# Earlier squares of the next block, paired log-sigmoids and two wide exponent activations in a hybrid attention, mLSTM and GLA layer

## The chip, the cores and the metric

The kernel runs on one core of one Trainium2 chip. The metric is device time in microseconds (us). Three runs of the kernel before gave 1427.89, 1430.01 and 1431.16 us; the median, 1430.01 us, is the time before.

## The reference

One layer over 2048 rows of width 1024. The rows are normalised (RMSNorm) and projected once; the columns of the projection feed three head groups, whose outputs are multiplied by gates, concatenated, projected back and added to the input. A last RMSNorm follows.

```python
hn = rmsnorm(x, norm_g)
z = einsum('bsd,de->bse', hn, w_in)
# A) softmax attention over a band of 9 chunks, with a relative-position bias
# B) mLSTM: exponential input gate, sigmoid forget gate, running-max stabiliser
lf = log_sigmoid(f_pre);  bcum = cumsum(lf)          # within a chunk
inter_log = bcum + m_prev
m_row = max(inter_log, max_j(log_d))
d_mat = exp(log_d - m_row);  inter_w = exp(inter_log - m_row)
den = max(abs(den), exp(-m_row))
# C) gated linear attention with a decay per key channel
log_alpha = log_sigmoid(ga @ w_alpha + b_alpha) / 16
```

What matters here are two log-sigmoids and a handful of exponentials. The forget gates of the six mLSTM heads are 6 rows (partitions) of numbers along time; the decays of GLA are 128 rows. From the forget and input gates come four rows per head, kept in one tile `rows`: gate minus cumulated decay, the weight of each key up to its chunk's end, exp(-m), and the weight of the old state.

## The kernel before, in words

The sequence is cut into 4 blocks of 512 rows (`q` = 0 to 3). The first phase, up to about 1005 us, does for each block the projections, mLSTM and GLA; the second phase does attention and the output projection. All the change is in the first phase.

For each block the order of projections is: `gq` and `gk` for GLA (`proj_z`), the row tiles of v (`proj_v`, eight of them, the first four with line 402 to 405 as their evacuation), the GLA gate, the mLSTM q and k, the mLSTM gates, then the nine attention tiles (`proj_a`). Each tile of a projection is 24 matmuls of 512 columns into one PSUM bank; there are two such banks (`ip`), so tile n+2 waits until tile n is copied out. Weights are read by DMA, split into a rounded part (line 235, ScalarE) and a rest (line 236, VectorE or GpSimd).

Between these matmuls smaller chains of work are woven in. They are generators with the names prep, gates, gla_in, gla and mlstm. Every `yield pe, gap` says how much TensorE time the piece before takes and how long the next piece should stay away; `flow.piece` hands out pieces at every half tile. This sets the order on TensorE, which is fixed by hand. The order on the other engines is set by a scheduler, which may put an instruction as early as its buffers and inputs allow, so that a line's place in the program isn't its place on its engine. Each engine then works strictly in its own order: one instruction that waits holds up all behind it.

The chains that the change touches:

- prep, for the next block: loads x in four tiles `xraw` (line 284), squares and sums them (line 285, ScalarE), forms the reciprocal root (286, 287) and a diagonal matrix (290), yields with a gap of 14, broadcasts it with a matmul (293), copies that (295), loads x transposed (299), scales it (302), and takes the gate columns with eight matmuls (309) into `g1` (314). The `xraw` tiles are four, shared by both loads.
- split_x: rounded part and rest of x for the projections (323, 324).
- gates: matmul 331 brings the 6 + 6 gate rows, line 272 to 276 (`log_sigmoid`) turn the forget rows into log-sigmoids: absolute value, minimum with 0, exp, ln(1 + .), difference. Scans follow (337 for the running maximum, 341 for the sums within a chunk), then the rows (342 to 353), the last of them by eight activations of one chunk each with a bias (352, 353). Then matmul 362 brings the 128 GLA rows, which pass through the same `log_sigmoid` into `ls`. After a gap, four transposes (369) read all of `rows`.
- gla_in: line 608 on, exponentials and scans of `ls`; they need `ls` and `zg`.

ScalarE reads its functions from a table that it has to load: exp and ln alternate here, and the loads stand as rows of their own, ACT_TABLE_LOAD.

In the text, B0 to B3 are the starts of the four blocks, and T1 to T4 the first four row tiles of v there. The two tiles ahead of T1 are gq (copied out by line 422) and gk (copied out by line 423).

Of the kernel before, what the change touches and what calls it, by code (L numbers as in the profile page):

```python
# [8 lines left out]
FP32 = mybir.dt.float32  # L9
FR = mybir.dt.float32r  # L10
AF = mybir.ActivationFunctionType
ALU = mybir.AluOpType
# [4 lines left out]
P = 128  # L17
D = 1024
KT = D // P
QT = 512  # L20
ST = 256
L = 128
NC = QT // L
AH, MH, GH = 6, 6, 4
# [3 lines left out]
G0 = 96  # L28
# [71 lines left out]
def f32(ap):  # L100
    return ap.bitcast(FP32)
# [3 lines left out]
def trunk_kernel(ctx: ExitStack, tc: tile.TileContext, xT, x, w_f, w_t, w_o, w_gates, norm_g, conv_w,  # L105
                 gate_sel, one_row, bias, ml_g, gla_g, final_g, out):
    nc = tc.nc
    S = x.shape[0]
    NQ = S // QT
# [23 lines left out]
    flow = Flow()  # L133
# [8 lines left out]
    with ExitStack() as pa_:  # L142
# [21 lines left out]
        gsel = one.tile([P, 2 * P], FP32, name="gsel")  # L164
# [3 lines left out]
        rows = one.tile([P, QT], FP32, name="rows")  # L168
# [44 lines left out]
        st = {"zb": None, "m": zero6, "S": None, "B": None}  # L213

        def g_tile(shape):
            return gpool.tile(shape, FP32, name="g")
# [50 lines left out]
                        flow.piece(12 * 0.227)  # L267
                evac(tt, ps)

        def log_sigmoid(dst, src, n):  # L270
            ab = g_tile([P, QT])[0:n] if n == P else g_tile([P, QT])[G0:G0 + n]
            nc.scalar.activation(ab, src, AF.Abs)
            nc.vector.tensor_scalar(dst, src, 0.0, None, op0=ALU.min)
            nc.scalar.activation(ab, ab, AF.Exp, scale=-1.0)
            nc.scalar.activation(ab, ab, AF.Ln, bias=1.0)
            nc.vector.tensor_tensor(dst, dst, ab, op=ALU.subtract)


        def prep(q, R):
            t0 = q * QT  # L280
            rs = big.tile([P, NC], FP32, name="rs")
            for tt in range(NC):
                xt = xraws.tile([P, D], FP32, name="xraw")
                nc.sync.dma_start(xt, x[t0 + tt * P:t0 + (tt + 1) * P, :])
                nc.scalar.activation(xt, xt, AF.Square, accum_out=rs[:, tt:tt + 1])
            nc.vector.tensor_scalar(rs, rs, 1.0 / D, EPS, op0=ALU.mult, op1=ALU.add)
            nc.gpsimd.tensor_tensor(rs, rs, mhalf[:, 0:NC], op=ALU.pow)
            dg = g_tile([P, NC, P])
            for tt in range(NC):
                nc.vector.tensor_scalar(dg[:, tt, :], ident, rs[:, tt:tt + 1], None, op0=ALU.mult)  # L290
            yield 0.0, 14.0
            rb = bank("pw")
            nc.tensor.matmul(rb, ones, dg.rearrange("p a t -> p (a t)"), start=True, stop=True)
            rbs = g_tile([P, QT])
            nc.scalar.copy(rbs, rb)
            raws = []
            for g in range(4):
                raw = xraws.tile([P, 2, QT], FP32, name="xraw")
                nc.sync.dma_start(raw, xT[:, 2 * g:2 * g + 2, t0:t0 + QT])
                for j in range(2):  # L300
                    k = 2 * g + j
                    nc.vector.scalar_tensor_tensor(raw[:, j, :], raw[:, j, :], ng[:, k:k + 1], rbs, op0=ALU.mult, op1=ALU.mult)
# [12 lines left out]
            R["raws"], R["g1"] = raws, g1  # L315
# [12 lines left out]
        def gates(q, g1, R):  # L328
            t0 = q * QT
            pb = bank("pw")  # L330
            nc.tensor.matmul(pb, gsel[:, P:2 * P], g1, start=True, stop=True)
            fm = g_tile([P, QT])[G0:G0 + MH]
            gi = g_tile([P, QT])[G0:G0 + MH]
            nc.vector.tensor_copy(gi, pb[32:32 + MH])
            log_sigmoid(fm, pb[0:MH], MH)
            mr = g_tile([P, QT])[G0:G0 + MH]
            nc.vector.tensor_tensor_scan(mr, fm, gi, st["m"], op0=ALU.add, op1=ALU.max)
            bc = g_tile([P, QT])[G0:G0 + MH]
            for c in range(NC):
                cs = slice(c * L, (c + 1) * L)  # L340
                nc.vector.tensor_tensor_scan(bc[:, cs], ones[G0:G0 + MH], fm[:, cs], 0.0, op0=ALU.mult, op1=ALU.add)
            nc.vector.tensor_tensor(rows[0:MH], gi, bc, op=ALU.subtract)
            nm = bc
            nc.vector.tensor_tensor(nm, bc, mr, op=ALU.subtract)
# [17 lines left out]
            nc.tensor.matmul(pa, gsel[:, 0:P], g1, start=True, stop=True)  # L362
            ls = big.tile([P, QT], FP32, name="ls", bufs=1)
            log_sigmoid(ls, pa, P)
            R["ls"] = ls
            yield 0.9, 13.0
            rt_ps = bank("pw")
            for c in range(NC):
                nc.tensor.transpose(out=rt_ps[:, c * P:(c + 1) * P], in_=rows[:, c * L:(c + 1) * L], identity=ident)
# [12 lines left out]
            yield 0.6, 1.0  # L382
# [351 lines left out]
        for q in range(NQ):  # L734
            st["q"] = q
            flow.need("gla_in")
            flow.need("gla")
            z = proj_z(X)
            vs, vg = proj_v(X)
            gg = proj_gg(X)  # L740
            flow.need("gates")
            G = {}
            flow.start("gla_in", gla_in(q, z, R["ls"], G))
            flow.start("gla", gla(q, vg, gg, G))
            flow.need("mlstm")
            qk = proj_m(X)
            M = dict(R)
            flow.start("mlstm", mlstm(q, qk, vs, M))
            M["gm"] = proj_gm(X)
            if q + 1 < NQ:  # L750
                flow.need("gla_in")
                R = {}
                flow.start("prep", prep(q + 1, R))
            proj_a(q, X)
            if q + 1 < NQ:
                flow.need("prep")
                X = split_x(R["raws"])
                flow.start("gates", gates(q + 1, R["g1"], R))
# [313 lines left out]
```

## Time and profile before

| | us |
|---|---|
| median of three runs | 1430.01 |
| the profiled execution, its own time | 1430.58 |
| its span in the trace | 1428.9 |
| TensorE busy | 1319.6 |
| VectorE busy | 788.7 |
| ScalarE busy | 616.5 |
| GpSimd busy | 606.5 |

The mean granted clock of TensorE is 0.953 of full speed. In rows of the profile PE is TensorE, PEld its weight loads, DVE is VectorE, ACT is ScalarE, POOL is GpSimd and SP the engine that issues most DMAs. A row of waits reads: engine, tile and line that waited, what ended the wait, total, how many times, the longest. A row of the timeline reads: start, duration, engine, line, operation, and in brackets the idle time ahead of it with what ended it.

### The profile page before, as it was taken

Reading aid. Unit: us, or ns where it says so; the run is one execution under the profiler, and the core shown is the slowest. Engines: PE = TensorE matmul, PEld = TensorE weight load, DVE = VectorE, ACT = ScalarE, POOL = GpSimd, SP = SyncE. Lnnn points to the kernel's source line nnn. Section 1 sums busy time; section 2 is a strip of 40 time slices with the busy share of each in tenths; the row PEclk is TensorE's granted clock in tenths of the full one; section 3 lists DMA queues with packets and bytes.
Section 4 is the critical chain, followed back from the end, with each engine's and each line's share of the span. In section 5 each row is a group of like instructions: output and inputs, shape, how many; then the busy total and the mean of one; then the engine's idle time right before and its main releaser. Section 6 shows DMA issues by size and latency. Waiting matters only on the chain.

```text
span 1428.9 us, 20086 instructions
## 1 busy us (share of the span) xinstructions
PE 1319.6 (92%) x7044; PEld 1064.9 (75%) x7044; DVE 788.7 (55%) x1874; ACT 616.5 (43%) x1173; POOL 606.5 (42%) x847
## 2 busy tenths in 40 slices
PE   5899989989998998999899899998878999999997
PEld 2678768867877876888677677787756887877876
DVE  6525556662664765265566527556556756656731
ACT  5634313463432347343224534321456555655531
POOL 4215762322576222266622325651245354454452
PEclk7999989999999999999999999997877999999999
DMA  7433214453421445432244533231587464555322
GB/s 245 152 112 117 74 54 131 133 177 111 118 74 56 130 140 177 125 111 74 67 124 121 156 118 93 73 110 49 148 241 229 130 184 133 179 161 160 99 67 89
DMA packets 107205, 180.10 MB, mean 126 GB/s; under 512 B 9824, under 2 KB 54752, under 8 KB 107104
## 3 DMA queue, kind: packets, MB, share of 16 engines
q1 hardware_dynamic: 102496, 170.43, 40.4%
q10 hardware_dynamic: 4608, 8.39, 1.6%
q8 instruction: 56, 0.92, 0.3%
q14 instruction: 45, 0.37, 0.1%
HBM read 143.14 MB, written 35.65 MB: 125 GB/s over the span
## 4 chain that ended last, share of the span: by engine, by line
PE 67%; DVE 12%; ACT 8%; DMA 6%; issue 4%; POOL 3%; SPq 0%; POOLq 0%; ACTq 0%; DVEq 0%
PE ip L243 11%; PE ip L245 10%; PE ip L244 10%; PE s L826 3%; PE ip L947 3%; PE ip L946 3%; PE ip L945 3%; PE ip L263 3%; PE ip L264 3%; PE ip L265 3%; PE tp L887 2%; DVE pt L840 2%; PE ga L673 2%; ACT w L235 2%; DVE qk L449 2%
## 5 line engine op out<-in xcount | busy, mean ns | idle before, releaser
L243 PE MATMUL ip<-x,w 128*128 128x512 f32 x800 | 326.7, 408 | 0.0
L244 PE MATMUL ip<-x,w 128*128 128x512 f32 x800 | 313.3, 392 | 1.2 <-DVE x L324 1.2
L245 PE MATMUL ip<-x,w 128*128 128x512 f32 x800 | 313.6, 392 | 0.0
L235 ACT CAST w<-wraw 128x1024 fp32r<-128x1024 f32 x132 | 138.3, 1049 | 193.9 <-PE ip L245 136.4
L236 DVE TENSOR_TENSOR w<-wraw,w 128x1024 fp32r<-128x1024 f32 x88 | 114.2, 1299 | 172.1 <-ACT w L235 170.0
L236 POOL TENSOR_TENSOR w<-wraw,w 128x1024 fp32r<-128x1024 f32 x44 | 106.1, 2410 | 217.5 <-ACT w L235 217.3
L243 PEld LDWEIGHTS ip<-x,w 128*128 128x128 f32 x800 | 150.9, 189 | 43.8 <-issue 11.9
L244 PEld LDWEIGHTS ip<-x,w 128*128 128x128 f32 x800 | 151.1, 189 | 32.8 <-DVE x L324 2.9
L245 PEld LDWEIGHTS ip<-x,w 128*128 128x128 f32 x800 | 150.7, 188 | 33.0
L845 POOL TENSOR_SCALAR pt<-pt,sm 128x640 f32<-128x640 f32 (+2 forms) x96 | 70.4, 735 | 148.8 <-DVE sm L844 118.1
L263 PE MATMUL ip<-w,x 128*128 128x512 f32 x256 | 105.5, 412 | 20.8 <-ACT zg L423 14.4
L264 PE MATMUL ip<-w,x 128*128 128x512 f32 x256 | 104.1, 407 | 4.6 <-POOL w L236 3.8
L945 PE MATMUL ip<-wo,y 128*128 128x512 f32 x256 | 107.0, 418 | 0.0
L843 ACT ACTIVATE pt<-pt,sm 128x640 f32<-128x640 f32 (+2 forms) x96 | 73.3, 764 | 71.0 <-DVE sm L840 68.0
L265 PE MATMUL ip<-w,x 128*128 128x512 f32 x256 | 103.3, 403 | 0.0
L947 PE MATMUL ip<-wo,y 128*128 128x512 f32 x256 | 101.7, 397 | 0.3 <-POOL y L853 0.3
L946 PE MATMUL ip<-wo,y 128*128 128x512 f32 x256 | 101.5, 396 | 0.0
L893 DVE TENSOR_TENSOR pl<-tp,ph 128x512 fp32r<-128x512 f32 (+2 forms) x126 | 74.6, 599 | 31.5 <-ACT ph L892 30.4
L826 PE MATMUL s<-kk,qq 128*128 128x384 f32 (+1 forms) x360 | 80.8, 333 | 10.7 <-DVE sm L840 9.2
L826 PEld LDWEIGHTS s<-kk,qq 128*128 128x128 f32 x360 | 60.6, 201 | 29.9 <-DVE sm L840 23.4
L633 POOL TENSOR_TENSOR prd<-gk,zg 128x16 f32<-128x16 f32 (+15 forms) x128 | 66.5, 520 | 33.4 <-PE pw L639 26.5
L892 ACT CAST ph<-tp 128x512 fp32r<-128x512 f32 (+2 forms) x126 | 63.1, 509 | 33.6 <-PE tp L887 32.4
(240 smaller groups left out, 2418.8 us busy)
## 6 DMA issues: line engine op xcount, KB each, us to landing
wraw<-in_w_f SPq DMA_DIRECT2D x100, 512.0 KB, 3.6
wraw<-in_w_t SPq DMA_DIRECT2D x32, 512.0 KB, 4.2
qq<-q_d SPq DMA_DIRECT2D x48, 256.0 KB, 4.5
kk<-k_d SPq DMA_DIRECT2D x18, 512.0 KB, 6.4
vv<-v_d SPq DMA_DIRECT2D x18, 512.0 KB, 7.3
xraw<-in_x SPq DMA_DIRECT2D x16, 512.0 KB, 4.6
xraw<-in_xT SPq DMA_DIRECT2D x16, 512.0 KB, 7.5
xr<-in_x SPq DMA_DIRECT2D x16, 512.0 KB, 3.7
```

What stands on the lines that cost most here:

```text
L235: nc.scalar.copy(w[:, :, 0, :], rv)
L236: other().tensor_tensor(w[:, :, 1, :], rv, f32(w[:, :, 0, :]), op=ALU.subtract)
L243: nc.tensor.matmul(ps, w[:, k, 0, :], X[k][:, 0, :], start=(k == 0), stop=False)
L244: nc.tensor.matmul(ps, w[:, k, 0, :], X[k][:, 1, :], start=False, stop=False)
L245: nc.tensor.matmul(ps, w[:, k, 1, :], X[k][:, 0, :], start=False, stop=(k == KT - 1))
L263: nc.tensor.matmul(ps, X[k][:, 0, t], w[:, 0, :], start=(k == 0), stop=False)
L264: nc.tensor.matmul(ps, X[k][:, 0, t], w[:, 1, :], start=False, stop=False)
L265: nc.tensor.matmul(ps, X[k][:, 1, t], w[:, 0, :], start=False, stop=(k == KT - 1))
L826: nc.tensor.matmul(sp[:, :cn], qq[:, l, tt * P:(tt + 1) * P], kk[:, ko + c0:ko + c0 + cn], start=(l == 0), stop=(l == 1))
L945: nc.tensor.matmul(ps, Y[k][:, 0, t], wo[k, j][:, 0, :], start=(e == 0), stop=False)
L946: nc.tensor.matmul(ps, Y[k][:, 0, t], wo[k, j][:, 1, :], start=False, stop=False)
L947: nc.tensor.matmul(ps, Y[k][:, 1, t], wo[k, j][:, 0, :], start=False, stop=(e == KT - 1))
```

## The change

Three edits. The part of prep up to the diagonal matrix becomes a function `prep_x` of its own, which is called for the next block ahead of the mLSTM projections instead of behind the mLSTM gates; prep then begins with the broadcast matmul, and its gap of 14 is gone. Both log-sigmoids of gates are taken together: both matmuls first, then the absolute values and exponentials of both, then both logarithms. The eight chunk activations become two of 512 columns: the chunk's bias is added before by VectorE with a broadcast operand (one addition for the key weights, two for the state weights), and three more rows are formed in a tile of their own and copied. The scheduler puts all of it in its own order.

```diff
-        def log_sigmoid(dst, src, n):
-            ab = g_tile([P, QT])[0:n] if n == P else g_tile([P, QT])[G0:G0 + n]
-            nc.scalar.activation(ab, src, AF.Abs)
-            nc.vector.tensor_scalar(dst, src, 0.0, None, op0=ALU.min)
-            nc.scalar.activation(ab, ab, AF.Exp, scale=-1.0)
-            nc.scalar.activation(ab, ab, AF.Ln, bias=1.0)
-            nc.vector.tensor_tensor(dst, dst, ab, op=ALU.subtract)
-        def prep(q, R):
+        def log_sigmoid(pairs):
+            for dst, src, ab in pairs:
+                nc.scalar.activation(ab, src, AF.Abs)
+                nc.vector.tensor_scalar(dst, src, 0.0, None, op0=ALU.min)
+                nc.scalar.activation(ab, ab, AF.Exp, scale=-1.0)
+            for dst, src, ab in pairs:
+                nc.scalar.activation(ab, ab, AF.Ln, bias=1.0)
+                nc.vector.tensor_tensor(dst, dst, ab, op=ALU.subtract)
+        def prep_x(q):
...
-            yield 0.0, 14.0
+            return dg
+
+        def prep(q, R, dg):
+            t0 = q * QT
+            yield 0.0, 0.0
...
             nc.vector.tensor_copy(gi, pb[32:32 + MH])
-            log_sigmoid(fm, pb[0:MH], MH)
+            nc.scalar.copy(fm, pb[0:MH])
+            yield 0.9, 3.0
+            pa = bank("pw")
+            nc.tensor.matmul(pa, gsel[:, 0:P], g1, start=True, stop=True)
+            ls = big.tile([P, QT], FP32, name="ls", bufs=1)
+            log_sigmoid([(ls, pa, g_tile([P, QT])), (fm, fm, g_tile([P, QT])[G0:G0 + MH])])
+            R["ls"] = ls
...
-            nc.vector.tensor_tensor(rows[0:MH], gi, bc, op=ALU.subtract)
             nm = bc
+            gb_ = gi
+            nc.vector.tensor_tensor(gb_, gi, bc, op=ALU.subtract)
+            nc.scalar.copy(rows[0:MH], gb_)
+            nc.scalar.activation(rows[64:64 + MH], mr, AF.Exp, scale=-1.0)
             nc.vector.tensor_tensor(nm, bc, mr, op=ALU.subtract)
             nc.scalar.copy(hl_nm[G0:G0 + MH], nm)
+            nc.vector.tensor_tensor(c4(gb_), c4(gb_), c4(nm)[:, :, L - 1:L].broadcast_to([MH, NC, L]), op=ALU.add)
+            nc.scalar.activation(rows[32:32 + MH], gb_, AF.Exp)
...
-            nc.scalar.activation(rows[64:64 + MH], mr, AF.Exp, scale=-1.0)
-            for c in range(NC):
-                cs = slice(c * L, (c + 1) * L)
-                mp = st["m"] if c == 0 else mr[:, c * L - 1:c * L]
-                nc.scalar.activation(iw[:, cs], nm[:, cs], AF.Exp, bias=mp)
-                nc.scalar.activation(rows[32:32 + MH, cs], rows[0:MH, cs], AF.Exp, bias=nm[:, (c + 1) * L - 1:(c + 1) * L])
+            nc.vector.tensor_tensor(iw[:, 0:L], nm[:, 0:L], st["m"].broadcast_to([MH, L]), op=ALU.add)
+            nc.vector.tensor_tensor(c4(iw)[:, 1:NC], c4(nm)[:, 1:NC], c4(mr)[:, 0:NC - 1, L - 1:L].broadcast_to([MH, NC - 1, L]),
+                                    op=ALU.add)
+            nc.scalar.activation(iw, iw, AF.Exp)
...
-            yield 0.9, 3.0
-            pa = bank("pw")
-            nc.tensor.matmul(pa, gsel[:, 0:P], g1, start=True, stop=True)
-            ls = big.tile([P, QT], FP32, name="ls", bufs=1)
-            log_sigmoid(ls, pa, P)
-            R["ls"] = ls
             yield 0.9, 13.0
...
-        flow.start("prep", prep(0, R))
+        flow.start("prep", prep(0, R, prep_x(0)))
         load_consts()
...
             flow.need("mlstm")
+            if q + 1 < NQ:
+                dg = prep_x(q + 1)
             qk = proj_m(X)
...
-                flow.start("prep", prep(q + 1, R))
+                flow.start("prep", prep(q + 1, R, dg))
```

How it moves instructions is read at three places. From here on lines of the changed kernel are called N and a number: N287 is before's 285 (squares), N341 the new copy of the 6 forget rows, N273, N275 and N277 are the absolute value, exp and ln of `log_sigmoid`, N278 its difference, N432 and N433 are before's 422 and 423, N414 is 404, N369 the last wide activation. In the rows as they stand below the letter is L in both.

First place: ScalarE at B1, from the squares to the copy of gk. Before:

```order
L285 ACTIVATE xraw,rs<-xraw 128x1024
L235 CAST w<-wraw 128x2x512
L422 ACTIVATE zg<-ip 128x512
L275 ACT_TABLE_LOAD
L275 ACTIVATE g<-g 6x512
L272 ACTIVATE g<-pw 128x512
L274 ACT_TABLE_LOAD
L274 ACTIVATE g<-g 128x512
L348 ACTIVATE rows<-g 6x512
L275 ACT_TABLE_LOAD
L275 ACTIVATE g<-g 128x512
L235 CAST w<-wraw 128x2x512
```

Line 423 follows. Now:

```order
L432 ACTIVATE zg<-ip 128x512
L287 ACTIVATE xraw,rs<-xraw 128x1024
L273 ACTIVATE g<-pw 128x512
L273 ACTIVATE g<-g 6x512
L275 ACTIVATE g<-g 128x512
L275 ACTIVATE g<-g 6x512
L277 ACT_TABLE_LOAD
L277 ACTIVATE g<-g 128x512
L277 ACTIVATE g<-g 6x512
L235 CAST w<-wraw 128x2x512
L433 COPY zg<-ip 128x512
```

One table load stands between the two copies where there were three; the 6-row absolute value and exp, which stood among the squares, now stand between the copies, and so does the fourth square. The squares themselves are where they were, behind split_x at the block's start. In the whole program the table loads are 9 where they were 17.

Second place: ScalarE just behind it, up to the end of the work on `rows`. Before, the last two of the eight chunk activations and what follows them:

```order
L352 ACTIVATE rows<-g 6x128
L353 ACTIVATE rows<-rows,g 6x128
L614 ACTIVATE qt<-lc 128x256 x2
L402 COPY vg<-ip 128x128
L404 CAST hl<-ip 128x3x64
```

Now:

```order
L359 ACTIVATE rows<-g 6x512
L412 COPY vg<-ip 128x128
L414 CAST hl<-ip 128x3x64
L628 ACTIVATE lc<-lc 128x256 x2
L358 COPY rows<-g 6x512
L674 COPY Qb<-qt 32x8x16 x4
L414 CAST hl<-ip 128x3x64
L361 CAST hl_nm<-g 6x512
L412 COPY vg<-ip 128x128
L363 ACTIVATE rows<-g 6x512
L414 CAST hl<-ip 128x3x64
L369 ACTIVATE rows<-rows 6x512
```

`rows` was complete ahead of the first copy of T1 (402); it now is complete behind the first copy of T2 (the second 412).

Third place: VectorE from the 6-row log-sigmoid on. Before, the 6-row chain was taken without a break:

```order
L276 TENSOR_TENSOR g<-g 6x512
L337 SCALAR_TENSOR_TENSOR g<-g,ml 6x512
L341 SCALAR_TENSOR_TENSOR g<-ones,g 6x128 x4
L273 TENSOR_SCALAR ls<-pw 128x512
L355 COPY ml<-g 6x1
L342 TENSOR_TENSOR rows<-g 6x512
```

Now, its head:

```order
L278 TENSOR_TENSOR g<-g 6x512
L622 SCALAR_TENSOR_TENSOR lc<-rst_153,ls 128x256 x2
L349 SCALAR_TENSOR_TENSOR g<-g,ml 6x512
L353 SCALAR_TENSOR_TENSOR g<-ones,g 6x128
L236 TENSOR_TENSOR w<-wraw,w 128x2x512
L353 SCALAR_TENSOR_TENSOR g<-ones,g 6x128 x3
L292 TENSOR_SCALAR g<-ident,rs 128x128 x4
```

Then come five short rows, N357 (before's 342), and this, up to the last addition to `rows`:

```order
L415 TENSOR_TENSOR hl<-ip,hl 128x3x64
L630 TENSOR_TENSOR qt<-zg,qt 128x256
L634 TENSOR_TENSOR Dt<-Dt,dl 128x2
L629 TENSOR_TENSOR lc<-lc,zg 128x256 x2
L360 TENSOR_TENSOR g<-g 6x512
L634 TENSOR_TENSOR Dt<-Dt,dl 128x2x2 x2
L415 TENSOR_TENSOR hl<-ip,hl 128x3x64
L362 TENSOR_TENSOR g<-g 6x512
L366 TENSOR_TENSOR rows<-g,ml 6x128
L367 TENSOR_TENSOR rows<-g 6x384
```

The GLA rows (622, 627, 630, 629: before's 612, 617, 620, 619), the split of a weight tile (236) and T1's copies (415, before's 405) now stand inside the 6-row chain, which has grown by three rows (362, 366, 367).

On TensorE the four transposes 369 stand where they stood, between T2 and T3. The broadcast matmul 293 and the gate matmuls 309 move some 14 us of modelled TensorE time earlier inside the block, and with them, on VectorE, the eight scalings 302.

More of the change, by code (lines that the diff above doesn't have):

```diff
@@ L268, in proj_t @@
                 evac(tt, ps)
-        def log_sigmoid(dst, src, n):
-            ab = g_tile([P, QT])[0:n] if n == P else g_tile([P, QT])[G0:G0 + n]
-            nc.scalar.activation(ab, src, AF.Abs)
-            nc.vector.tensor_scalar(dst, src, 0.0, None, op0=ALU.min)
-            nc.scalar.activation(ab, ab, AF.Exp, scale=-1.0)
-            nc.scalar.activation(ab, ab, AF.Ln, bias=1.0)
-            nc.vector.tensor_tensor(dst, dst, ab, op=ALU.subtract)
-        def prep(q, R):
+        def log_sigmoid(pairs):
+            abs_ = []
+            for dst, src, ab in pairs:
[6 more added lines that the diff above has]
+        def prep_x(q):
             t0 = q * QT
@@ L331, in gates @@
             nc.tensor.matmul(pb, gsel[:, P:2 * P], g1, start=True, stop=True)
+            gi = g_tile([P, QT])[G0:G0 + MH]
             fm = g_tile([P, QT])[G0:G0 + MH]
-            gi = g_tile([P, QT])[G0:G0 + MH]
             nc.vector.tensor_copy(gi, pb[32:32 + MH])
-            log_sigmoid(fm, pb[0:MH], MH)
+            nc.scalar.copy(fm, pb[0:MH])
[5 more added lines that the diff above has]
+            R["ls"] = ls
             mr = g_tile([P, QT])[G0:G0 + MH]
@@ L341, in gates @@
                 nc.vector.tensor_tensor_scan(bc[:, cs], ones[G0:G0 + MH], fm[:, cs], 0.0, op0=ALU.mult, op1=ALU.add)
-            nc.vector.tensor_tensor(rows[0:MH], gi, bc, op=ALU.subtract)
+            c4 = lambda t: t.rearrange("p (c t) -> p c t", t=L)
             nm = bc
+            gb_ = gi
+            nc.vector.tensor_tensor(gb_, gi, bc, op=ALU.subtract)
+            nc.scalar.copy(rows[0:MH], gb_)
+            nc.scalar.activation(rows[64:64 + MH], mr, AF.Exp, scale=-1.0)
             nc.vector.tensor_tensor(nm, bc, mr, op=ALU.subtract)
             nc.scalar.copy(hl_nm[G0:G0 + MH], nm)
+            nc.vector.tensor_tensor(c4(gb_), c4(gb_), c4(nm)[:, :, L - 1:L].broadcast_to([MH, NC, L]), op=ALU.add)
+            nc.scalar.activation(rows[32:32 + MH], gb_, AF.Exp)
             nc.vector.tensor_tensor(hl_nm[32:32 + MH], nm, f32(hl_nm[G0:G0 + MH]), op=ALU.subtract)
             iw = rows[G0:G0 + MH]
-            nc.scalar.activation(rows[64:64 + MH], mr, AF.Exp, scale=-1.0)
-            for c in range(NC):
-                cs = slice(c * L, (c + 1) * L)
-                mp = st["m"] if c == 0 else mr[:, c * L - 1:c * L]
-                nc.scalar.activation(iw[:, cs], nm[:, cs], AF.Exp, bias=mp)
-                nc.scalar.activation(rows[32:32 + MH, cs], rows[0:MH, cs], AF.Exp, bias=nm[:, (c + 1) * L - 1:(c + 1) * L])
+            nc.vector.tensor_tensor(iw[:, 0:L], nm[:, 0:L], st["m"].broadcast_to([MH, L]), op=ALU.add)
+            nc.vector.tensor_tensor(c4(iw)[:, 1:NC], c4(nm)[:, 1:NC], c4(mr)[:, 0:NC - 1, L - 1:L].broadcast_to([MH, NC - 1, L]),
+                                    op=ALU.add)
+            nc.scalar.activation(iw, iw, AF.Exp)
             ml = big.tile([P, 1], FP32, name="ml")[G0:G0 + MH]
```

## The prediction

> **What bounds the kernel.** I read the engines' totals, then TensorE's waits, then the clock by windows, then the timelines of ScalarE and TensorE at the block starts.
>
> ```profile
> PE 1319.6 (92%) x7044; PEld 1064.9 (75%) x7044; DVE 788.7 (55%) x1874; ACT 616.5 (43%) x1173; POOL 606.5 (42%) x847
> ```
>
> TensorE is busy for 1319.6 of 1428.9 us. Its matmuls stay, so the change can win only idle time of TensorE, or clock. Time saved on ScalarE counts where TensorE waits for it.
>
> ```profile
> PE ip L263 <- ACT zg L423: 14.4, 4, 5.1
> PE pw L362 <- DVE g L273: 2.2, 1, 2.2
> ```
>
> The first row is the copy of gk, late once in each block; the second stands at B0. The matmuls that ended the waits at B0, B1 and B2, in this order (the bracket is the idle time ahead):
>
> ```profile
> 54.59 0.50 PE L263 MATMUL ip<-w,x 128*128 128x512 f32 x1 [2.58 <-ACT zg L423]
> 64.28 0.50 PE L263 MATMUL ip<-w,x 128*128 128x512 f32 x1 [1.87 <-DVE hl L405]
> 295.75 0.50 PE L263 MATMUL ip<-w,x 128*128 128x512 f32 x1 [0.42 <-ACT zg L422]
> 305.06 0.79 PE L263 MATMUL ip<-w,x 128*128 128x512 f32 x1 [3.54 <-ACT zg L423]
> 314.71 0.71 PE L263 MATMUL ip<-w,x 128*128 128x512 f32 x1 [2.11 <-DVE hl L405]
> 552.64 0.50 PE L263 MATMUL ip<-w,x 128*128 128x512 f32 x1 [3.12 <-ACT zg L423]
> 562.28 0.50 PE L263 MATMUL ip<-w,x 128*128 128x512 f32 x1 [1.85 <-DVE hl L405]
> ```
>
> T2 waits for gk's copy, then T3 for T1's copies. Idle time costs twice, as windows of 3.4 us show (after the first pair of columns come TensorE's busy time, and near the end the granted clock):
>
> ```profile
> 304.60:308.00 3.40, 2.94 (x7) 2.36 (x8) 3.34 (x5) 3.33 (x6) 2.69 (x4) 0.50 0.22 20
> 311.40:314.80 3.40, 1.29 (x9) 0.89 (x7) 3.25 (x17) 3.02 (x12) 0.90 (x3) 1.00 0.02 5
> 314.80:318.20 3.40, 3.40 (x8) 2.64 (x9) 2.72 (x17) 0.32 (x1) 1.27 (x4) 0.50 0.41 116
> 560.60:564.01 3.41, 1.73 (x8) 1.44 (x9) 3.33 (x20) 1.45 (x6) 2.16 (x7) 1.00 0.23 70
> 564.01:567.42 3.41, 3.41 (x17) 2.83 (x16) 1.08 (x6) 0.32 (x1) 0.00 (x0) 1.00 0.47 136
> ```
>
> The window after the wait for gk's copy is granted 0.50, and so is the one after 1.29 us of work; after one with 1.73 us the next stays at 1.00. The limit lies near half, and a halved window costs half of itself, 1.7 us. The whole block starts show how many there are:
>
> ```profile
> 40.00:70.00 30.00, 23.29 (x86) 17.71 (x86) 19.91 (x55) 22.94 (x44) 9.63 (x18) 0.89 0.41 130
> 534.00:565.00 31.00, 26.03 (x106) 20.15 (x105) 20.35 (x58) 24.91 (x48) 10.24 (x18) 0.94 0.58 197
> 778.00:832.00 54.00, 46.99 (x198) 37.48 (x197) 25.01 (x62) 27.90 (x54) 15.66 (x30) 0.94 0.55 150
> ```
>
> 30 us x 0.11 = 3.3 us lost at B0 (two windows), 31 x 0.06 = 1.9 at B2 (one), 54 x 0.06 = 3.2 at B3 (two); at B1 the two above, 3.4. So the block starts cost now: B0 2.2 + 2.6 + 1.9 + 3.4 = 10.1; B1 0.4 + 3.5 + 2.1 + 3.4 = 9.5; B2 3.1 + 1.9 + 1.7 = 6.7; B3 5.1 + 3.4 = 8.5.
>
> **The change at B1, step by step.** ScalarE's rows ahead of gk's copy:
>
> ```profile
> 291.29 1.06 ACT L285 ACTIVATE xraw<-xraw 128x1024 f32<-128x1024 f32 x1 [1.48 <-DMA xraw<-in_x]
> 295.11 0.59 ACT L422 ACTIVATE zg<-ip 128x512 f32<-128x512 f32 x1
> 295.71 1.28 ACT L275 ACT_TABLE_LOAD   x1
> ```
>
> *Squares.* By the order of instructions they stay at the block start: the third is held by its DMA at 291.29 in either program. One moves behind gq's copy. I price the move at nothing by itself, and what it puts between the copies is counted below. Its DMAs stay beside those of the weights.
>
> *Paired log-sigmoids.* Before gq's copy one 6-row activation and one square fall away, 1.7 us, but the third square still ends at 292.4 and the weight's rounding (1.0 us) follows, so gq's copy ends at about 294.0 instead of 295.7; T1 no longer waits 0.4. Then stand the fourth square with its sum, 1.2, two absolute values and two exps, 4 x 0.6 like line 422, one load, 1.3: the first logarithm ends at about 299.4, the second at 300.0, then the rounding and gk's copy, to about 301.7. Before it was 305.0, just ahead of the matmul at 305.06: two loads of three are gone. T1, begun at 295.3, ends at 301.0 (T2 could start at 305.06 - 3.54 = 301.5 before, which is T1's 5.7 us from 295.75). So T2 waits 0.7 instead of 3.5, and ends 5.5 us later at 307.2.
>
> *Wide exponents, and what now stands in the chain to `rows`.* T3 stands behind the transposes of `rows` on TensorE, and these need N369. Before, `rows` was ready for them, and T1's copies were last. VectorE's chain in the new order runs from the first logarithm to N367, with these durations (groups by form; total, then mean ns):
>
> ```profile
> L236 DVE TENSOR_TENSOR w<-wraw,w 128x1024 fp32r<-128x1024 f32 x2 | 2.5, 1226 | 0.8 <-ACT w L235 0.8
> L612 DVE TENSOR_TENSOR_SCAN lc<-rst,ls 128x256 f32<-128x256 f32 x2 | 1.5, 773 | 0.0
> L341 DVE TENSOR_TENSOR_SCAN g<-ones,g 6x128 f32<-6x128 f32 x4 | 1.4, 394 | 0.0
> L337 DVE TENSOR_TENSOR_SCAN g<-g,ml 6x512 f32<-6x512 f32 x1 | 1.3, 1284 | 0.0
> L290 DVE TENSOR_SCALAR g<-ident,rs 128x128 f32<-128x128 f32 x4 | 0.9, 282 | 0.0
> L619 DVE TENSOR_TENSOR lc<-lc,zg 128x256 f32<-128x256 f32 x2 | 0.8, 422 | 0.1
> L405 DVE TENSOR_TENSOR hl<-ip,hl 128x192 fp32r<-128x192 f32 x4 | 1.4, 350 | 0.3 <-ACT hl L404 0.3
> L344 DVE TENSOR_TENSOR g<-g 6x512 f32<-6x512 f32 x1 | 0.7, 687 | 0.0
> ```
>
> Two differences 1.4, GLA scans 1.5, running maximum 1.3, chunk scans 1.4, the split weight 1.2, the diagonals 0.9, six rows like 619 2.4, two of 405 0.7, three of 512 columns like 344 2.1 (N357, N360, N362), N366 and N367 by their columns 0.8 and some eight tiny ones 0.4 in all beyond their overlap: 14.1. Neighbouring short rows overlap; I take off 1.0. So N367 ends at 299.4 + 13.1 = 312.5, and N369, one activation of 0.6, at 313.1. Eight activations are gone and one sits on the path in their place; the saving of width lies where nobody waits. The transposes wait from 307.2 to 313.1, 5.9, and T3 starts at about 313.7 instead of 314.71. Window 308.0 to 311.4 would be idle, so the rest until 314.8 goes at half clock: 0.9 lost. That window would hold about 1.8 us of work, by the 1.73 above just not halving the next. B1 costs 0.7 + 5.9 + 0.9 = 7.5: a gain of **2.0**. If it does halve, 0.3.
>
> **The other blocks.**
>
> ```profile
> 44.64 0.59 ACT L422 ACTIVATE zg<-ip 128x512 f32<-128x512 f32 x1
> 542.57 0.59 ACT L422 ACTIVATE zg<-ip 128x512 f32<-128x512 f32 x1
> 785.58 0.59 ACT L422 ACTIVATE zg<-ip 128x512 f32<-128x512 f32 x1
> 798.38 0.79 PE L263 MATMUL ip<-w,x 128*128 128x512 f32 x1 [5.13 <-ACT zg L423]
> 806.08 0.60 PE L369 MATMUL pw<-ident,rows 128*128 128x128 f32 x4
> ```
>
> From the end of gq's copy to where T2 could begin: B1 295.7 to 301.5, 5.8; B2 543.2 to 549.5, 6.3; B0 45.2 to 52.0, 6.8. TensorE comes later against the chain by the difference, so the wait for `rows` is shorter by it. B2: 5.9 - 0.5 = 5.4, first wait about 0.1, clock 0 to 1.7, I take 0.8; 6.3 against 6.7, gain **0.4**. B0: its 2.2 us wait for L273 goes too, which brings TensorE forward: 5.9 - 1.0 + 2.2 = 7.1, with a halved window 1.7 makes 8.8 against 10.1: gain **1.3**. B3 has no next block's squares. The first logarithm ends at 786.2 + 1.3 + 0.6 = 788.1, N369 13.7 later at 801.8; T2 starts unhindered at 798.38 - 5.13 = 793.2, ends at 798.7 and the wait is 3.1. The transposes run at 801.9 instead of 806.1, less 0.8 for a possible halved window: 3.4. Then weights come last, though:
>
> ```profile
> PE ip L264 <- POOL w L236: 1.9, 1, 1.9
> ```
>
> That wait (812 to 832) grows by what TensorE is earlier, unless the weights are earlier as well: between 0 and 3.4 stays, I take half, **1.7**.
>
> **What was added elsewhere.** At the start x's loads pass the small constant loads on SP, from L219 on:
>
> ```profile
> 2.16 0.66 SPq L219 DMA_DIRECT2D wg<-in_w_gates  x1
> ...
> 6.00 1.75 SPq L284 DMA_DIRECT2D xraw<-in_x  x4
> ```
>
> They can be 3.8 us earlier, but the transposed x stands behind weight loads in the new order, whose buffers free when they did: I take 0, between a gain of 3.8 and a loss of as much, if the constants now come last. In the middle of a block, broadcast 293 and the scaling 302 come some 14 us earlier, for which nobody waited (no such row beyond the start). But VectorE's order there now puts 683 behind six of 515, which wait for matmul 512; 690 on TensorE waits for 683:
>
> ```profile
> 257.93 0.86 DVE L515 SCALAR_TENSOR_TENSOR dd<-s,rt,cap 128x128 f32<-128x128 f32 x3
> 248.76 0.62 DVE L683 TENSOR_TENSOR at<-ga,at 128x448 f32<-128x448 f32 x1
> ```
>
> 2 x 0.86 + 0.62 = 2.3 us, beside half a tile of matmuls, 12 of them, 2.6 us at the 16 to 17 in 3.41 us above. Hidden if all starts together, 2.3 lost per block if nothing covers it; nearer the first, I take 0.6, in three blocks **1.8** lost.
>
> **Sum.** 2.0 + 0.4 + 1.3 + 1.7 - 1.8 = 3.6 us. The profiled execution took 1430.58, so 1427.0 by it; the median is 0.6 below that execution, 1426.4. I forecast **1426.5 us**. Of waits alone little changes: B0 to B2 wait 6.7 + 6.0 + 5.0 before and 7.1 + 6.6 + 5.5 after. The gain of these three is clock, two stretches of idle time joined into one.
>
> The Trainium skill ("TensorE: Matmul & The Clock Gate", Part 1: The HAM clock gate) has the clock fall to half after at least one idle window of about 3.4 us. The window with 1.29 us of work, followed by 0.50, disagrees if idle means without any work; the measurement decides. By the page, short waits before would have cost no clock and the joined one of 5.9 could, so that the sum would be waits alone: B0 to B2 lose 1.5, B3 gains 1.7, minus 1.8, a time of about 1431.6.
>
> **Rivals.**
> - *No measurable change, about 1429.1.* The clock isn't won: B1's window of 1.8 us is within 0.1 of one that held, and if it and B2's halve, 1.7 + 0.9 of the 3.6 go. For it: the waits alone don't shrink. Against: three stretches of two waits become one.
> - *Slower, about 1434.* The chain to N369 is longer than my sum. The same split on VectorE stands at 1.23 us in the groups and at 2.16 once, while GpSimd works on a split of its own,
>
> ```profile
> 326.57 2.16 DVE L236 TENSOR_TENSOR w<-wraw,w 128x1024 fp32r<-128x1024 f32 x1 [2.88 <-ACT w L235]
> ```
>
> 0.93 us more. The split stands in the chain now; stretched so at four places it costs 3.7 us, and the gain is gone: that is the point from which this decides. If the scans and additions beside GpSimd's work stretch by as much again, it is 4 x 1.9 = 7.6 us, 1426.5 + 7.6 = 1434.1. Against: in the groups above, read across B1, both splits were short.
> - *Larger gain, about 1418.* The overlaps are larger, or VectorE's short rows slip behind: a chain 2 us shorter in all four, with no halved window behind B0 or B2, gives 4 x 2 less, 1418.5. Against: I counted each row in the order it will have.
> - *The earlier squares do nothing.* Their DMAs hold them; already my price, so it changes no number.
>
> **Chances.** Forecast 0.44 (its own range 1423 to 1429, by B1's 1.7, B3's half and the 690 term); no change 0.24; slower 0.20; larger gain 0.12. A measurement here tells about 0.2%, 2.9 us, from no change, so forecast splits: three quarters of it (0.33) and the larger gain are faster, 0.45; the rest of it and the second case same, 0.35; slower 0.20. Range 1420 to 1434: it reaches up towards the third case and down towards the fourth and leaves out about 0.2.
>
> **What would show it.** Right: the waits on 423 (then 433) nearly gone; a new row at four places of the transposes (369, N379) waiting for ScalarE's `rows`, 5 to 7 us at B0 to B2 and about 3 at B3; table loads 9 instead of 17; one halved window at a block start instead of two. Wrong: T3 later than before at B1, 690 waiting over 1 us for 683, or squares that stand clear of the block starts.

## The result: slower by 0.8%

| | us |
|---|---|
| changed kernel, median of 7 runs | 1441.83 (1435.50 to 1445.19) |
| before, beside it, median of 7 runs | 1430.01 (1427.89 to 1432.06) |
| ratio | 1.0079, 95% interval 1.0058 to 1.0100 |
| profiled execution of the changed kernel | 1441.83, span 1439.9 |
| forecast | 1426.5, range 1420 to 1434 |

The time lies above the whole range. Lines of the changed kernel stand below as its own profile has them: L379 are the transposes (before's 369), L369 the last wide activation, L433 gk's copy, L415 T1's subtracted copies (before's 405). The engines' totals and the head of TensorE's waits after:

```profile
PE 1322.5 (92%) x7044; PEld 1069.9 (74%) x7044; DVE 802.4 (56%) x1886; ACT 603.6 (42%) x1149; POOL 615.5 (43%) x847
...
PE pw L379 <- ACT rows L369: 27.8, 4, 7.8
PE pw L299 <- DVE g L292: 10.1, 1, 10.1
PE s L532 <- DVE qk L462: 5.5, 4, 2.1
PE ip L263 <- ACT zg L433: 0.5, 1, 0.5
```

Of gk's copy 14.4 us have become 0.5, as intended. In their place TensorE waits 27.8 us at four places for `rows`, and T1's copies, which took 5.8 us before, are behind that wait and no longer named. The four waits, B0 to B3 in this order:

```profile
63.73 1.11 PE L379 MATMUL pw<-ident,rows 128*128 128x128 f32 x4 [7.82 <-ACT rows L369]
315.66 1.12 PE L379 MATMUL pw<-ident,rows 128*128 128x128 f32 x4 [7.22 <-ACT rows L369]
567.29 1.12 PE L379 MATMUL pw<-ident,rows 128*128 128x128 f32 x4 [7.16 <-ACT rows L369]
815.47 1.11 PE L379 MATMUL pw<-ident,rows 128*128 128x128 f32 x4 [5.60 <-ACT rows L369]
```

Forecast were 7.1, 5.9, 5.4 and 3.1. B1 by windows, with the granted clock as the number ahead of the last two:

```profile
306.30:309.70 3.40, 2.14 (x10) 1.45 (x8) 3.27 (x13) 0.62 (x2) 1.57 (x5) 1.00 0.53 154
309.70:313.20 3.50, 0.00 (x0) 0.00 (x0) 3.41 (x12) 2.78 (x8) 0.55 (x2) 0.99 0.00 0
313.20:316.60 3.40, 0.94 (x5) 0.94 (x6) 3.25 (x13) 2.48 (x7) 0.76 (x4) 0.50 0.42 118
316.60:320.00 3.40, 3.40 (x10) 2.63 (x10) 1.89 (x12) 0.03 (x1) 0.89 (x3) 0.50 0.39 116
```

While TensorE stands idle for a whole window, VectorE (third pair of columns) is busy for 3.41 of 3.50 us: ScalarE, whose last row TensorE waits for, waits itself for VectorE. Two windows are halved, not one.

### The profile page after: what moved, and what is told of

The parts are those of the page before. It is cut to its first block, busy times and chain, and to the rows that moved or that the text cites. A ratio compares the mean times of both kernels' runs of the same rounds, so it can differ in the third digit from the quotient of the medians.

```text
span 1439.9 us, 20049 instructions
## 1 busy us (share of the span) xinstructions
PE 1322.5 (92%) x7044; PEld 1069.9 (74%) x7044; DVE 802.4 (56%) x1886; ACT 603.6 (42%) x1149; POOL 615.5 (43%) x847
## 4 chain that ended last, share of the span: by engine, by line
PE 58%; DVE 17%; DMA 8%; ACT 7%; issue 5%; POOL 4%; SPq 1%; POOLq 0%; ACTq 0%; DVEq 0%
PE ip L243 9%; PE ip L245 8%; PE ip L244 8%; DVE qk L459 3%; PE s L838 3%; PE ip L959 3%; PE ip L957 3%; PE ip L958 3%; ACT w L235 2%; PE ip L264 2%; PE tp L899 2%; PE ip L265 2%; PE ip L263 2%; DVE pt L852 2%; PE ga L683 2%
## 5 line engine op out<-in xcount | busy, mean ns | idle before, releaser
L264 PE MATMUL ip<-w,x 128*128 128x512 f32 x256 | 102.9, 402 | 4.7 <-POOL w L236 3.9
L263 PE MATMUL ip<-w,x 128*128 128x512 f32 x256 | 104.6, 408 | 0.9 <-ACT zg L433 0.5
L265 PE MATMUL ip<-w,x 128*128 128x512 f32 x256 | 102.3, 400 | 0.0
L459 DVE SCALAR_TENSOR_TENSOR qk<-u,cw,qk 128x512 f32<-128x512 f32 x72 | 67.7, 940 | 17.5 <-ACT qk L457 15.5
```

The source lines that it names most:

```text
L263: nc.tensor.matmul(ps, X[k][:, 0, t], w[:, 0, :], start=(k == 0), stop=False)
L264: nc.tensor.matmul(ps, X[k][:, 0, t], w[:, 1, :], start=False, stop=False)
L265: nc.tensor.matmul(ps, X[k][:, 1, t], w[:, 0, :], start=False, stop=(k == KT - 1))
```

## The experiments

Twelve kernels, each against the kernel before on the same chip. Ratios with 95% intervals:

| | edits | median us | ratio |
|---|---|---|---|
| e1 | first (earlier squares) | 1422.64 | 0.9939 (0.9919 to 0.9960) |
| e2 | second (pairing) | 1438.28 | 1.0043 (1.0022 to 1.0063) |
| e3 | third (wide exponents) | 1429.16 | 0.9980 (0.9963 to 0.9998) |
| e5 | second, third | 1440.66 | 1.0081 (1.0056 to 1.0106) |
| e6 | first, second | 1439.16 | 1.0063 (1.0044 to 1.0081) |
| e7 | first, third | 1420.28 | 0.9931 (0.9905 to 0.9956) |
| e8 | all three, measured again | 1441.07 | 1.0087 (1.0054 to 1.0119) |
| e4 | all three, transposes behind T4 | 1425.20 | 0.9963 (0.9946 to 0.9979) |
| e11 | all three, the 6 rows first in the pair | 1423.31 | 0.9963 (0.9946 to 0.9979) |
| e9 | first, at the start only | 1424.37 | 0.9966 (0.9950 to 0.9981) |
| e10 | first, in the loop only | 1428.22 | 0.9995 (0.9978 to 1.0013) |
| e12 | first, third, gk copied by VectorE | 1421.24 | 0.9940 (0.9920 to 0.9961) |

**The theories.** The chain theory: pairing puts other work into the chain that makes `rows`, and TensorE waits for it. The rival, moved prep: in the profiled run the stretches at the block starts account for only about a third of the lost 11 us (4.2, counted from gk's first matmul to the first one behind T8), the middle of the blocks for most of the rest, and that is where the first edit moved the broadcast and the scaling.

### Each edit alone, and the chain cut

e1 is the first edit alone, e2 the second, e3 the third. Their cores:

```diff
 e1
-            yield 0.0, 14.0
+            return dg
...
+            if q + 1 < NQ:
+                dg = prep_x(q + 1)
             qk = proj_m(X)
 e2
-            log_sigmoid(fm, pb[0:MH], MH)
+            log_sigmoid([(ls, pa, g_tile([P, QT])), (fm, fm, g_tile([P, QT])[G0:G0 + MH])])
 e3
-                nc.scalar.activation(iw[:, cs], nm[:, cs], AF.Exp, bias=mp)
+            nc.scalar.activation(iw, iw, AF.Exp)
 e4, in the changed kernel
-            yield 0.9, 13.0
+            yield 0.9, 24.0
```

> The kernel before with the first edit alone (squares of the next block called a stage sooner). Chain theory (the loss comes from the rows chain behind the paired log-sigmoids): 1430, within 2 us, waits at the block starts as before (gk's copy 14.4 us, no wait of the transposes). Moved-prep theory (in the profiled run only about 4 of the 11 us arose between the copies of gq and T4, 7 in the middle of the blocks, where the broadcast and scaling of prep now stand): 1436 or more, with the extra time between 150 and 290 us of each block.

> The kernel before with the second edit alone (both log-sigmoids together; the eight chunk activations stay). Chain theory: 1438 to 1443, gk's copy no longer waited for, the transposes wait 6 to 8 us for ScalarE's rows at B0 to B2, since VectorE's order puts the scans of GLA, a weight's split and T1's copies into the 6-row chain. Moved-prep theory: 1428 to 1431.

> The kernel before with the third edit alone (two wide activations and a copied tile). Both theories: 1429 to 1433. gk's copy is a little later, because two copies of 0.6 us stand ahead of it, and the wait for it grows from 14.4 to 17 to 19 us in all; rows is ready early, the transposes do not wait.

> The changed kernel with the gap ahead of the transposes 24 instead of 13, so that they stand behind T4 on TensorE; VectorE's and ScalarE's orders stay. Chain theory: the 27.8 us of waits of the transposes go, T3 waits instead for T1's copies, which end 2.4 us ahead of rows at B1: 2 to 3 us less at each block start and fewer halved windows, 1430 to 1434. Moved-prep theory: 1439 or more.

Measured: 0.9939, 1.0043, 0.9980 and 0.9963. Moved prep falls as the cause: the first edit alone makes the kernel faster, by 0.6%, which neither theory expected, and its profile is 4.1 us ahead of before's in the middle of the blocks. The pairing alone makes it slower, with the wait that the chain theory named:

```profile
PE pw L371 <- ACT rows L361: 26.1, 16, 6.2
```

(L371 are the transposes of e2, four to a block, each of which waits for its own chunk; L361 are the chunk activations of the key weights, which e2 keeps. The profile is of e2's fastest execution, 1430.77 us. Up to the last projection tile it is 6.4 us behind the profile of before; the second phase, where the program is the same, came out 6.2 us shorter.) In e3 the wait for gk's copy did not grow to 17 to 19 us as expected: it is 10.8 us in all, where before had 14.4. In e4 the orders of VectorE and ScalarE up to `rows` are those of the changed kernel, and the table loads stay at nine; on TensorE the transposes have moved. It is faster than before, and some 16 us faster than the changed kernel, more than the chain theory had expected. Its waits at the block starts:

```profile
PE ip L263 <- DVE hl L415: 21.8, 4, 6.4
```

So 27.8 us become 21.8: now it is T1's copies, further ahead in the same VectorE order, that T3 waits for. At B1 the wait is 4.9 where it was 7.2. Up to the last projection tile e4's profile is 13.8 us ahead of the changed kernel's: 8.1 at the four block starts, 4.0 in the middle of block 1, where a loss described below is gone with the other order on GpSimd, the rest in small amounts.

### Pairs of edits

e5, e6 and e7 join the diffs of two edits; e8 is the changed kernel again.

> Second and third edit without the first. The three edits alone gave -8.8, +6.8 and -2.3 us, together they cost 11.8: one pair interacts by some 16. Additive: 1436. If pairing and wide exponents are what interacts (three more rows of VectorE and a copy inside a chain that is now waited for): 1444 or more, with a wait of the transposes clearly over e2's 26 us.

> First and second edit without the third. Additive: 1429.5. If the first edit and pairing are what interacts (squares that now stand between the copies of gq and gk hold the logarithms, and the earlier prep no longer helps): 1438 to 1442.

> First and third edit without the pairing. Additive, and by the chain theory: 1420 to 1422, the fastest so far, no wait of the transposes. If the first edit and the wide exponents interact: 1430 or more.

> The changed kernel as it is, beside the others on the same chip. All theories: 1438 to 1444, as measured first. Its second profile shows which of the losses of the first come again: the waits of the transposes, 27.8 us in all, by the chain theory to within 2 us; halved windows elsewhere may differ.

Measured: 1.0081, 1.0063, 0.9931 and 1.0087. The eight combinations read so (ratio, without and with pairing):

| | without | with | pairing adds |
|---|---|---|---|
| neither of the others | 1 | 1.0043 | 0.0043 |
| first | 0.9939 | 1.0063 | 0.0124 |
| third | 0.9980 | 1.0081 | 0.0101 |
| first and third | 0.9931 | 1.0087 | 0.0156 |

Pairing loses in every row, between 6 and 22 us of 1430. First and third edit add up without it (0.9939 x 0.9980 = 0.992, measured 0.9931); with it, neither gains anything. e5 came out between its two cases. Longer waits for `rows` are not what takes the gain of the first edit: they are 26.1 us in e2 and in e6, 27.9 in e5 and in e8 (longest 7.8), 27.8 in the changed kernel.

TensorE's projection tiles come in the same order in all profiles, so their starts show where the time goes. At the block starts, from gk's first matmul to the first one behind T8, all four together, in us against before (one profile each):

| | without | with | pairing adds |
|---|---|---|---|
| neither of the others | 0 | +6.6 (e2) | 6.6 |
| first | -2.8 (e1) | +8.6 (e6) | 11.4 |
| third | -0.2 (e3) | +9.9 (e5) | 10.1 |
| first and third | -5.7 (e7) | +4.2 (changed), +5.3 (e8) | 9.9, 11.0 |

So pairing costs 7 to 11 us at the block starts whatever stands beside it. What it costs beyond that lies mostly at two places in the middle of blocks: 3.0 us in block 1 of e6, e8 and the changed kernel, and 3.8 us in block 2 of e4, e5, e8 and the changed kernel. Both have to do with GpSimd and are described below.

### Which row of the pair comes first

```diff
-            log_sigmoid([(ls, pa, g_tile([P, QT])), (fm, fm, g_tile([P, QT])[G0:G0 + MH])])
+            log_sigmoid([(fm, fm, g_tile([P, QT])[G0:G0 + MH]), (ls, pa, g_tile([P, QT]))])
```

> The changed kernel with the two log-sigmoids paired the other way round, the 6 forget rows first. VectorE then has the running maximum and the chunk scans ahead of GLA's scans, and T1's copies behind the rows chain; but a table load and an exp stand ahead of gk's copy (1.9 us). Chain theory: the wait of the transposes falls from 27.8 to under 15 us, gk's copy and T1's copies are waited for again; 1430 to 1438. If it is not VectorE's order in the chain that costs: 1441 as before.

Measured: 1423.31, ratio 0.9963, below the expected 1430 to 1438; two entries of a list changed over are worth about 18 us. B1 of e11, on VectorE, ScalarE and TensorE:

```profile
296.38 0.69 DVE L278 TENSOR_TENSOR g<-g 6x512 f32<-6x512 f32 x1 [1.77 <-ACT g L277]
...
308.30 0.55 DVE L367 TENSOR_TENSOR rows<-g 6x384 f32<-6x384 f32 x1
```

```profile
300.88 1.28 ACT L359 ACT_TABLE_LOAD   x1
302.17 0.62 ACT L359 ACTIVATE rows<-g 6x512 f32<-6x512 f32 x1
...
308.96 0.62 ACT L369 ACTIVATE rows<-rows 6x512 f32<-6x512 f32 x1
```

```profile
304.40 0.80 PE L263 MATMUL ip<-w,x 128*128 128x512 f32 x1 [5.36 <-ACT zg L433]
312.51 0.60 PE L379 MATMUL pw<-ident,rows 128*128 128x128 f32 x4
```

`rows` is complete at 309.6, and the transposes at 312.5 wait for nothing; over the program they wait once, 1.2 us, at B0. The reading has a limit: the scheduler, given this order, also separates the logarithms again, so that the table loads are 17 as before, and gk's copy is waited for 12.8 us in all. So e11 doesn't isolate VectorE's order from the pairing itself, and it also lacks both losses in the middle of the blocks. At the block starts its profile is 6.6 us ahead of the changed kernel's (-2.4 against +4.2): there the place of the 6-row chain is worth more than 8 table loads, 10 us of ScalarE. No run here has nine loads with the 6-row scans first.

### Where the first edit gains

```diff
 e9: prep_x(0) ahead of load_consts(), for later blocks as before
+                dg = prep_x(q)
+                yield 0.0, 14.0
 e10: block 0 as before, prep_x(q + 1) ahead of proj_m
+                dg = prep_x(q + 1)
             qk = proj_m(X)
 e12: first and third edit, and
-            nc.scalar.copy(z[:, 1, :], proj_f("gk", X))
+            nc.vector.tensor_copy(z[:, 1, :], proj_f("gk", X))
```

> The first edit split: only the start of the program changes (x's loads of block 0 ahead of the constants), in the loop the squares stay with prep where they were. If the 8 us that the first edit gains come from the start and B0 (TensorE's 2.2 us wait for line 273 there and what follows): 1424 to 1426. If they come from the blocks' ends: 1429 to 1431.

> The other half of the first edit: squares of the next block called ahead of the mLSTM projections, and the gap of 14 gone, but the start as before. If the gain lies in the loop (x transposed loaded earlier, so that its split no longer holds a matmul at the block's end, 0.5 and 0.7 us and what halved windows follow): 1424 to 1427. If it lies at the start: 1429 to 1431.

> First and third edit without the pairing, and gk copied out by VectorE instead of ScalarE, so that no table load stands ahead of it. Leaves nothing out. By the waits of the kernel without this (gk's copy 9.6 us, T1's copies 4.5 us): if the copy alone was late, most of 9.6 us goes and T1's copies take some of it back, 1411 to 1417; if VectorE is as late as ScalarE, 1420.

Measured: 0.9966, 0.9995 and 0.9940. The gain comes with the edit of the start; the loop half, the one that the change is named after, can't be told from nothing. (Together they make 0.9961, where e1 has 0.9939, a difference of the size of the intervals.) TensorE's waits in the window from 30 to 70 us, before and in e9:

```profile
PE ip L263 <- ACT zg L423: 2.6, 1, 2.6
PE pw L362 <- DVE g L273: 2.2, 1, 2.2
PE ip L263 <- DVE hl L405: 1.9, 1, 1.9
PE pw L309 <- DVE xraw L302: 0.6, 1, 0.6
```

```profile
PE ip L263 <- DVE hl L413: 3.6, 1, 3.6
PE pw L317 <- DVE xraw L310: 1.8, 1, 1.8
```

7.3 us are 5.4, and the wait for line 273 is gone. That is 1.9 of the 5 us; single profiles differ by as much as 5 us in their last 400 us, where the program is the same (from the start of the last projection tile 396.0 us before, 390.8 in e9), so where the rest lies stays open. e12 moves gk's copy to VectorE, and VectorE is as late with it (e7, with ScalarE's copy, waits 9.6 us):

```profile
PE ip L263 <- DVE zg L431: 10.7, 4, 4.2
```

Of the kernels tried, e7 has the lowest time, 1420.28 us; the ratios of e1 and e12 lie inside its interval. All three leave out the pairing.

## Why the prediction was wrong, step by step

The forecast was 15.3 us too low. By the profile of the changed kernel, 9.6 us of that arose at the block starts, where 5.4 us were forecast as gained and 4.2 were lost (from gk's first matmul to the first one behind T8), and 4.5 in the middle of the blocks, where 1.8 us were forecast as lost and 6.3 were (3.6 in e8's profile).

**What bounds the kernel: right, but not all of it.** It is idle time of TensorE and the clock behind it, at the block starts and also in the middle of blocks.

**Paired log-sigmoids, gk's copy: right.** At B1 T2 waits 0.5, forecast 0.7. The chain began as forecast too: the changed kernel reaches B1 later by 1.4,

```profile
285.00 1.02 PE L331 MATMUL pw<-g,gsel 128*128 128x512 f32 x2
```

```profile
286.36 1.02 PE L337 MATMUL pw<-g,gsel 128*128 128x512 f32 x2
```

(the same matmul before and after), and its first logarithm was ready for VectorE at 300.45, which is 299.1 less that shift; forecast 299.4.

**The chain to `rows`: the step that failed first, by a term of 1.0 us at B1.** VectorE's first and last row of it, and ScalarE's last, at B1 of the changed kernel:

```profile
300.45 0.69 DVE L278 TENSOR_TENSOR ls<-ls,g 128x512 f32<-128x512 f32 x1 [2.76 <-ACT g L277]
...
314.10 0.55 DVE L367 TENSOR_TENSOR rows<-g 6x384 f32<-6x384 f32 x1
```

```profile
314.98 0.63 ACT L369 ACTIVATE rows<-rows 6x512 f32<-6x512 f32 x1
```

From 300.45 to 314.65 it is 14.2 us; the rows that I added came to 14.1, and I then took off 1.0 for overlap. The overlap was there for some neighbours only: the running maximum (303.20, 1.28 long) and the first chunk scan (304.41) overlap by 0.07, while the two differences, the GLA scans and the running maximum stand 0.02 to 0.04 apart, and what the short rows gain these lose again. ScalarE, busy with line 414, took up its last row 0.3 later; the transposes came at 315.66, or 314.3 less the shift, not 313.1, and T3 at 316.43, less the shift 315.1, against 314.71 before: later, not 1.0 earlier. I had named the point from which the gain is gone, a stretch of 0.93 us at four places, and had an overlap of that size in the sum as a gain.

**Clock: too kind.** I let 1.8 us of work fall into the window that ends at 314.8 and the next stay whole. The window behind the idle one held 0.94, and the next was halved too (316.60, 0.50). B1 costs 0.5 + 7.2 idle and, with two windows at half clock, 0.5 us more than before, in place of a gain of 2.0. From gk's first matmul to the first one behind T8 the granted clock was halved for 3, 2, 3 and 1 windows from B0 to B3 (e8: 4, 2, 2 and 2), where before had 2, 2, 1 and 2; the sum had one at B0 and at B1 and half of one at B2 and at B3.

**B0, B2 and B3: the carry-over was too kind.** For B0 and B2 I took B1's wait and corrected it by TensorE's own shift, which gave 7.1 and 5.4; measured are 7.8 and 7.2. For B3 I put one table load and one logarithm, 1.9 us, between gq's copy and the first logarithm's end; it was 5.9 (794.95 to 800.82), and the wait was 5.6 instead of 3.1. B3's gain of 1.7 went with it (0.1 lost). And at B0 and B3 a row of the chain is stretched, the GLA scans, beside a weight's split of GpSimd. The scans at B1, B3 and B0 and the two splits:

```profile
301.89 1.27 DVE L622 TENSOR_TENSOR_SCAN lc<-rst,ls 128x256 f32<-128x256 f32 x2
802.26 3.43 DVE L622 TENSOR_TENSOR_SCAN lc<-rst,ls 128x256 f32<-128x256 f32 x2
49.37 3.44 DVE L622 TENSOR_TENSOR_SCAN lc<-rst,ls 128x256 f32<-128x256 f32 x2
```

```profile
802.59 2.55 POOL L236 TENSOR_TENSOR w<-wraw,w 128x1024 fp32r<-128x1024 f32 x1 [15.09 <-ACT w L235]
49.70 2.57 POOL L236 TENSOR_TENSOR w<-wraw,w 128x1024 fp32r<-128x1024 f32 x1 [6.33 <-ACT w L235]
```

At both places 1.27 us are 3.4, in a chain that TensorE waits for. All six kernels that pair with the 128 rows first (e2, e4, e5, e6, e8 and the changed one) show it at both. Before's scans at B0 take 3.50 us as well, but they stand behind VectorE's last row for `rows`.

**Line 690: the right place, priced too high.** Forecast were 1.8 lost; in the changed kernel the waits at this place are 0.8 us in all, where before had 0.3:

```profile
PE ga L700 <- DVE at L693: 0.8, 2, 0.5
```

**The start: priced at nothing, its edit gained 0.34%.** e9 is 0.9966 (0.9950 to 0.9981), a gain of 2.7 to 7.2 us. I held the transposed x, behind the weights, for the only thing that counts at the start, and took TensorE's 2.2 us wait at B0 for a part of the gates alone. The gates of block 0 come after prep, and prep begins with the squares.

**The loop half of the first edit: right**, nothing (e10).

**What wasn't in the prediction: the middle of the blocks, and GpSimd's order.** In the changed kernel a memset of GLA's tile stands two products earlier on GpSimd than in e4, and waits there for VectorE:

```profile
454.64 0.23 POOL L632 MEMSET Dt<- 128x162 f32 x1 [2.74 <-DVE Sst L713]
```

```profile
446.77 0.23 POOL L632 MEMSET Dt<- 128x162 f32 x1 [0.46 <-DVE Sst L713]
```

(the same memset in block 1, changed kernel and e4). The products behind it come late, TensorE waits 2.7 us for them where before had 2.0, and three more windows are halved there. From the start of the projection tile at 436.4 (before's 434.6) to that of the next, the profiles take 28.0 us in the changed kernel, in e6 and in e8, 24.1 to 25.1 in before and the other ten: 3.0 us lost. Another 3.8 us go in block 2, where a VectorE row and a split of GpSimd collide (line 462, below): the tile there takes 10.7 to 10.9 us in the changed kernel, e4, e5 and e8, 7.0 in all others. The prediction had neither; I had read the orders of VectorE, ScalarE and SP, not that of GpSimd.

**The rivals.** "Slower, about 1434" had the mechanism, a longer chain to N369, and a chance of 0.20. Its reason was half right: VectorE's split in the chain stayed at 1.23 at B1 and B2, but the GLA scans were stretched by GpSimd at B0 and B3, 2.2 us each. For the block starts alone its 1434 was near (1430.6 + 4.2); it was too low since it counted nothing outside them. "The earlier squares do nothing" holds for the loop, not for the start. The 1431.6 worked out by the rule of the Trainium skill, from waits alone, was nearer by luck: partly idle windows went on being halved (below), and the losses in the middle of the blocks were not in it.

## What to carry to other kernels

Before work of two chains is joined to save an engine some set-up, look which of the two is waited for, and by whom: here the 128-row chain that nobody waited for was put ahead of the 6-row one, and TensorE waited 27.8 us for the latter. A sum of rows along an engine's order should not have overlap taken off where the rows depend on each other, and a forecast whose gain goes with that one correction has no sign. Where a scheduler sets the orders, a change in one place moves rows on engines that it doesn't touch; read all of them.

## What the runs showed of the hardware

**VectorE and GpSimd can exclude each other for a whole instruction.** Line 462 (before's 452), a 128x512 operation of VectorE, and GpSimd's weight split. Before, VectorE starts 0.02 us ahead; in the changed kernel 0.05 us behind:

```profile
650.18 0.69 DVE L452 SCALAR_TENSOR_TENSOR qk<-e,qk 128x512 f32<-128x512 f32 x1 [1.72 <-ACT e L451]
```

```profile
650.20 2.91 POOL L236 TENSOR_TENSOR w<-wraw,w 128x1024 fp32r<-128x1024 f32 x1
```

```profile
658.46 2.84 DVE L462 SCALAR_TENSOR_TENSOR qk<-e,qk 128x512 f32<-128x512 f32 x1 [1.57 <-ACT e L461]
```

```profile
658.41 2.34 POOL L236 TENSOR_TENSOR w<-wraw,w 128x1024 fp32r<-128x1024 f32 x1
```

Whoever comes second is recorded longer by about the other's rest: 0.69 becomes 2.84, 2.34 becomes 2.91. It shows as duration, not as a wait. The GLA scans above are the same case. TensorE then waits 2.06 us for line 462. The changed kernel, e4, e5 and e8 lose this race (the line takes 855 to 864 ns in the mean there, 765 to 772 in the others). Not every pair does it: in the changed kernel GpSimd's line 676, begun at 176.58 us beside VectorE's line 693 (176.55, 0.62 long), took 0.37 us, as elsewhere. The Trainium skill ("SBUF — State Buffer", Terms) says that the two share a pair of ports which one of them holds for its full instruction while the other blocks; the four rows agree.

**The limit for half clock isn't one number of busy time.** In the prediction a window with 1.73 us of work left the next whole. In the changed kernel:

```profile
442.90:446.31 3.41, 1.70 (x16) 1.46 (x14) 2.41 (x8) 2.28 (x3) 2.97 (x3) 1.00 0.00 0
446.31:449.72 3.41, 3.41 (x23) 2.92 (x21) 1.74 (x7) 0.76 (x4) 3.22 (x9) 0.50 0.68 195
...
453.14:456.55 3.41, 1.84 (x22) 1.10 (x21) 1.59 (x5) 0.38 (x1) 1.83 (x4) 1.00 0.00 0
456.55:459.96 3.41, 2.24 (x9) 1.65 (x9) 0.42 (x1) 0.00 (x0) 3.10 (x6) 0.50 0.00 0
459.96:463.40 3.44, 3.44 (x25) 3.20 (x24) 1.27 (x3) 0.14 (x1) 2.75 (x5) 0.50 0.00 0
```

After 1.70 us in 16 matmuls the next window is halved, after 1.84 us in 22 as well, and after 2.24 us at half clock; after 1.73 us in 8 large ones it was not. What is counted can't be told from these runs. The page of the Trainium skill that the prediction cites speaks of idle windows; none of these was wholly idle.
